# The one-hot rows of the gate matrix, stored one token after another instead of four tokens interleaved

## The chip, the core and the metric

The kernel runs on one core of one Trainium2 chip. The core has a matrix engine (TensorE, PE in the profile; its weight loads are listed apart as PEld), a vector engine (VectorE, DVE), an activation engine (ScalarE, ACT), GpSimd (POOL) and a queue for transfers on SyncE (SP). The engines run side by side, each through its own list of instructions in order, and wait for one another through semaphores. The metric is the device time of one execution in microseconds (us); lower is better.

## The reference

The program is a two-layer decoder on 512 tokens of width 1024. Layer 0 mixes tokens by retention, layer 1 by differential attention; behind each stands an expert feed-forward network with 16384 experts (PEER). Only that network matters here:

```python
sc = jnp.einsum('thpd,hpnd->thpn', q, subkeys)      # two scores per head, 128 keys each
s1, i1 = lax.top_k(sc[:, :, 0], 16)
s2, i2 = lax.top_k(sc[:, :, 1], 16)
cand = s1[..., :, None] + s2[..., None, :]          # the best 16 of these pairs
idx = i1 * 128 + i2                                 # 8 heads x 16 = 128 experts a token
gate = softmax(top)
act = gelu(einsum('ted,td->te', u[idx], xc))
out = einsum('te,ted->td', gate * act, v[idx])
```

So each token uses 128 of 16384 experts, each with a gate. An expert's number is a pair of keys (a, b), both from 0 to 127.

## The kernel before

The 512 tokens are four blocks of 128. Block 0 is done sparsely: the rows of u and v that its tokens chose are gathered from memory, 128 experts at a time, by GpSimd (`sparse_u`, L735 to L743, and `sparse_v`), and VectorE multiplies them. The other 384 tokens are done densely: TensorE multiplies them with all of u and all of v, 128 experts (one value of a) at a time, and a matrix of gates, zero for experts that were not chosen, picks what counts.

That gate matrix is made by `gmat` (L798 to L835), called for each of the three dense blocks in each layer. For one token, its 128 chosen pairs lie along the partitions. `eq` (L820) compares them with 0 to 127 and gives two one-hot rows per pair, one for a and one for b, in bf16. These rows are widened to float32 in the tile `oh`: ScalarE copies the b half (L822), VectorE multiplies the a half with the gate (L823). Then one matmul per token (L827) with `oh[:, 1]` as weights and `oh[:, 0]` as the moving operand sums the 128 pairs into a 128 x 128 gate matrix in PSUM. Four tokens make a round and share a PSUM bank (`b`, of four with the tag "pj"); ScalarE copies the bank out (L830, L832), and every 16 tokens a transfer writes them to memory (L834). A layer has 96 rounds, the kernel 192. `oh` has four buffers (`OHB`) and `eq` two (`EQB`), so VectorE can be up to four rounds ahead of TensorE.

In both `eq` and `oh`, the last axis is the token within the round: element (a, token) lies at 4a + token. In `eq` that lets one comparison with `iota4` make two halves of four tokens at once. In `oh` it means that a matmul, which takes the 128 values of one token, reads one float32 of every four, a step of 16 bytes.

The order of the work around it is made in `peer` (L862 and on). `gates()` runs, for each of the three blocks, `topk_pairs` (L682 to L733: the best 16 pairs of each head, nearly all on VectorE) and then `gmat`. Both are generators that yield a cost, and between the yields `peer` places dense u tiles (`u_tile`, L837: a load, a split of the weights into a high and a low half on ScalarE at L92 and GpSimd at L93, 24 matmuls at L96 to L98 and a gelu at L843) and gathers for block 0 with their product on VectorE (L739, L741). The tiles of a generator step and of `u_tile` alternate by these costs, which are constants and do not depend on the change. The framework's scheduler then places the instructions of each engine. So in this first part of a layer TensorE alternates between rounds of L827 and u tiles, with three long stages of `gmat` and the `topk_pairs` of the next block between them. The second part of a layer multiplies with v and does not use `oh`. The scores' matmuls in `scores` (L793) are float32 too, 128 x 128, with both operands stored without a step.

`topk_pairs` takes its tile `tk_eq` from the same four buffers as `oh`.

Of the kernel before, what the change touches and what calls it, by code (L numbers as in the profile page):

```python
# [18 lines left out]
F32 = mybir.dt.float32  # L19
# [4 lines left out]
AF = mybir.ActivationFunctionType  # L24
OP = mybir.AluOpType
# [3 lines left out]
P = 128  # L29
# [24 lines left out]
OHB = 4  # L54
# [8 lines left out]
def build(tc, I, out):  # L63
    nc = tc.nc
    ctx = ExitStack()
    with ctx:
# [21 lines left out]
        def bank(tag):  # L88
            return psum.tile([P, 512], F32, name=tag, tag=tag, bufs=4 if tag == "pj" else 2)
# [708 lines left out]
        def gmat(kp, idx, gate, t0, gd, G0):  # L798

            ii = kp.tile([P, 2, P], I32, name="g_ii", tag="g_ii")  # L800
            nc.vector.tensor_scalar(out=ii[:, 0, :], in0=idx, scalar1=7, scalar2=None, op0=OP.arith_shift_right)
            nc.vector.tensor_scalar(out=ii[:, 1, :], in0=idx, scalar1=127, scalar2=None, op0=OP.bitwise_and)
            fi = kp.tile([P, 2, P], F32, name="g_if", tag="g_if")
            nc.vector.tensor_copy(out=fi, in_=ii)
            b = bank("rt")
            for i, src in enumerate((fi[:, 0, :], fi[:, 1, :], gate)):
                nc.tensor.transpose(b[:, i * P:i * P + P], src, ident)
            tr = kp.tile([P, 3, P], F32, name="g_tr", tag="g_tr")
            nc.vector.tensor_copy(out=tr.rearrange("p a b -> p (a b)"), in_=b[:, :3 * P])
            ks = kp.tile([P, 2, P], BF16, name="g_ks", tag="g_ks")  # L810
            nc.vector.tensor_copy(out=ks, in_=tr[:, 0:2, :])
            for q in range(P // GT):
                st = kp.tile([P, P - GA * NG0, GT], F32, name="g_st", tag="g_st", bufs=2)
                for r in range(GT // 4):

                    eq = kp.tile([P, 2, P, 4], BF16, name="g_eq", tag="g_eq", bufs=EQB)
                    oh = kp.tile([P, 2, P, 4], F32, name="g_oh", tag="g_oh", bufs=OHB)
                    tk = q * GT + r * 4
                    ts = slice(tk, tk + 4)
                    nc.vector.tensor_tensor(out=eq, in0=iota4[:, None].to_broadcast([P, 2, P, 4]),  # L820
                                            in1=ks[:, :, None, ts].to_broadcast([P, 2, P, 4]), op=OP.is_equal)
                    nc.scalar.activation(oh[:, 1], eq[:, 1], AF.Copy)  # L822
                    nc.vector.tensor_tensor(out=oh[:, 0], in0=eq[:, 0],  # L823
                                            in1=tr[:, 2, None, ts].to_broadcast([P, P, 4]), op=OP.mult)
                    b = bank("pj")
                    for i in range(4):
                        nc.tensor.matmul(b[:, i * P:i * P + P], oh[:, 1, :, i], oh[:, 0, :, i], start=True, stop=True)  # L827
                    b3 = b.rearrange("p (t a) -> p t a", t=4)
                    rs = slice(r * 4, r * 4 + 4)
                    nc.scalar.activation(st[:, :, rs].rearrange("p a t -> p t a"), b3[:, :, GA * NG0:], AF.Copy)  # L830
                    for i in range(NG0):
                        nc.scalar.activation(G0[i][:, t0 // GT + q, :, rs].rearrange("p a t -> p t a"),  # L832
                                             b3[:, :, GA * i:GA * i + GA], AF.Copy)
                nc.sync.dma_start(gd[t0 // GT + q], st.rearrange("p a t -> p (a t)"))  # L834
                yield 6.0  # L835
# [26 lines left out]
        def peer(l, norm, feed, prepare):  # L862
            with tc.tile_pool(name="sp", bufs=1) as sp, tc.tile_pool(name="dp", bufs=1) as dp:
# [6 lines left out]
                with tc.tile_pool(name="p1", bufs=1) as kp:  # L870
# [10 lines left out]
                    with tc.tile_pool(name="tk", bufs=1) as tp:  # L881
                        def gates():
                            for t in range(1, TB):
                                idx = tp.tile([P, P], I32, name="tk_idx", tag="tk_idx", bufs=2)
                                gate = tp.tile([P, 8, 16], F32, name="tk_g", tag="tk_g", bufs=2)
                                yield from topk_pairs(tp, M[t], MI[t], idx, gate)
                                yield from gmat(tp, idx, gate.rearrange("p h k -> p (h k)"), (t - 1) * P, gd, G0)

                        for _ in topk_pairs(tp, M[0], MI[0], idx0, gate0):
                            pass  # L890
                        su = sparse_u(sp, 0, l, idx0, act0)
                        nu, nd, tv, tu = 0, 0, 0.0, -40.0

                        for cost in gates():
                            tv += cost
                            while tu < tv and nu < P:
                                act = u_tile(dp, l, nu)
                                nc.sync.dma_start(ad[nu], act)
                                nu += 1
                                tu += UT  # L900
                                while nd < DOTS * (nu - LAG):
                                    next(su, None)
                                    nd += 1
                                    tv += 1.2
# [130 lines left out]
```

## Time and profile before

| what | value |
|---|---|
| runs of the kernel | 3529.66, 3531.1, 3543.05 us (median 3531.1) |
| the profiled execution | 3544.41 us, of which the span from first to last instruction is 3542.6 us |
| mean granted TensorE clock | 0.980 |
| instructions | 47177 |
| HBM read and written | 692.09 MB and 77.59 MB |

The page of the profile gives the busy time of each engine, a picture of the span in 40 slices of 88.6 us, the chain of work that ended last, and the costliest groups of instructions. A group is named by line, engine, operation and tiles (written<-read), with a count, the time in which any of its instructions ran, the mean length of one in ns, and the idle time of the engine just before them with what ended it. Each float32 matmul of the program shows as two MATMUL records and two LDWEIGHTS records, so the 768 matmuls of L827 are 1536 records. Records of matmuls overlap: the next one starts before the end of the last, so what a matmul costs in a run is the distance from start to start and not the length of a record.

### The profile page before, as it was taken

Reading aid. Unit: us, or ns where it says so; the run is one execution under the profiler, and the core shown is the slowest. Engines: PE = TensorE matmul, PEld = TensorE weight load, DVE = VectorE, ACT = ScalarE, POOL = GpSimd, SP = SyncE. Lnnn points to the kernel's source line nnn. Section 1 sums busy time; section 2 is a strip of 40 time slices with the busy share of each in tenths; the row PEclk is TensorE's granted clock in tenths of the full one; section 3 lists DMA queues with packets and bytes.
Section 4 is the critical chain, followed back from the end, with each engine's and each line's share of the span. In section 5 each row is a group of like instructions: output and inputs, shape, how many; then the busy total and the mean of one; then the engine's idle time right before and its main releaser. Section 6 shows DMA issues by size and latency. Waiting matters only on the chain.

```text
span 3542.6 us, 47177 instructions
## 1 busy us (share of the span) xinstructions
PE 3402.5 (96%) x16666; PEld 3047.2 (86%) x16666; DVE 2590.5 (73%) x4593; ACT 1401.1 (40%) x2436; POOL 1539.4 (43%) x919
## 2 busy tenths in 40 slices
PE   9999998799999999999999999879999999999998
PEld 7888888799999888899888668879999988889997
DVE  4444469987866888997673565998877588888776
ACT  3232333455454333333333543336445433333332
POOL 1110336544644333675533323453555433357653
PEclk9999999899999999999999999989999999999999
DMA  5222224756668999998753213366667799999884
GB/s 203 87 86 84 84 95 132 231 203 218 227 224 291 351 353 360 320 319 275 265 160 91 61 32 94 114 193 227 217 221 244 246 359 359 349 316 335 296 267 136
DMA packets 311486, 772.81 MB, mean 218 GB/s; under 512 B 25808, under 2 KB 153168, under 8 KB 311248
## 3 DMA queue, kind: packets, MB, share of 16 engines
q1 hardware_dynamic: 237520, 501.32, 41.8%
q0 software_dynamic: 73728, 268.47, 22.3%
q8 instruction: 131, 2.15, 0.2%
q14 instruction: 107, 0.88, 0.1%
HBM read 692.09 MB, written 77.59 MB: 217 GB/s over the span
## 4 chain that ended last, share of the span: by engine, by line
PE 79%; DVE 11%; DMA 3%; issue 3%; POOL 2%; ACT 1%; POOLq 0%; SPq 0%; DVEq 0%; ACTq 0%
PE pj L96 12%; PE pj L97 11%; PE pj L98 11%; PE pj L827 10%; PE mu L96 7%; PE mu L98 7%; PE mu L97 7%; PE rt L98 4%; PE rt L97 4%; PE rt L96 4%; DMA vg<-in_v,idx 2%; DVE tk_idf L725 2%; DVE tk_ex L722 1%; DVE scr L741 1%; POOL wl L93 1%
## 5 line engine op out<-in xcount | busy, mean ns | idle before, releaser
L93 POOL TENSOR_TENSOR wl<-wraw,wh 128x1024 fp32r<-128x1024 f32 x316 | 801.8, 2539 | 638.5 <-ACT wh L92 606.0
L92 ACT ACTIVATE wh<-wraw 128x1024 fp32r<-128x1024 f32 x632 | 659.9, 1053 | 704.9 <-issue 270.6
L96 PE MATMUL mu<-xth,wh 128*128 128x384 f32 (+1 forms) x2080 | 713.5, 343 | 23.6 <-ACT uact L843 23.5
L98 PE MATMUL mu<-xth,wl 128*128 128x384 f32 (+1 forms) x2080 | 708.0, 340 | 28.3 <-POOL wl L93 28.3
L97 PE MATMUL mu<-xtl,wh 128*128 128x384 f32 (+1 forms) x2080 | 706.2, 340 | 0.0
L93 DVE TENSOR_TENSOR wl<-wraw,wh 128x1024 fp32r<-128x1024 f32 x316 | 422.7, 1339 | 184.8 <-ACT wh L92 169.4
L739 POOL DMA_INDIRECT ug<-in_u,idx x256 | 312.1, 1219 | 470.1 <-DVE act L741 227.4
L752 POOL DMA_INDIRECT vg<-in_v,idx x256 | 320.7, 1253 | 408.2 <-DVE x L754 225.8
L754 DVE SCALAR_TENSOR_TENSOR x<-vg,wgt,x 128x1024 f32<-128x1024 f32 x256 | 399.2, 1559 | 111.0 <-DMA vg<-in_v,idx 109.6
L92 ACT ACTIVATE wwh<-w 128x384 fp32r<-128x384 f32 x256 | 134.4, 525 | 808.4 <-issue 388.2
L98 PEld LDWEIGHTS mu<-xth,wl 128*128 128x128 f32 x2080 | 397.3, 191 | 31.5 <-POOL wl L93 31.4
L96 PEld LDWEIGHTS mu<-xth,wh 128*128 128x128 f32 x2080 | 398.1, 191 | 30.3 <-ACT uact L843 26.8
L741 DVE CUSTOM_DVE_ANT_0 scr<-ug,x 128x1024 bf16<-128x1024 f32 x256 | 334.6, 1307 | 119.1 <-DMA ug<-in_u,idx 113.2
L97 PEld LDWEIGHTS mu<-xtl,wh 128*128 128x128 f32 x2080 | 398.4, 192 | 3.7
L97 PE MATMUL pj<-wl,wwh 128*128 128x512 f32 x1024 | 399.5, 390 | 0.0
L96 PE MATMUL pj<-wh,wwh 128*128 128x512 f32 x1024 | 399.2, 390 | 0.3 <-ACT wh L92 0.3
L827 PE MATMUL pj<-g_oh 128*128 128x128 f32 x1536 | 376.4, 417 | 23.4 <-DVE g_oh L823 13.8
L98 PE MATMUL pj<-wh,wwl 128*128 128x512 f32 x1024 | 397.8, 389 | 0.0
L827 PEld LDWEIGHTS pj<-g_oh 128*128 128x128 f32 x1536 | 367.1, 331 | 25.3 <-issue 14.3
L823 DVE TENSOR_TENSOR g_oh<-g_eq,g_tr 128x512 f32<-128x512 bf16 x192 | 188.3, 1005 | 98.6 <-PE pj L827 97.9
L93 DVE TENSOR_TENSOR wwl<-w,wwh 128x384 fp32r<-128x384 f32 x256 | 169.7, 664 | 104.5 <-ACT wwh L92 91.9
L98 PEld LDWEIGHTS pj<-wh,wwl 128*128 128x128 f32 x1024 | 192.3, 188 | 40.5
(241 smaller groups left out, 5624.3 us busy)
## 6 DMA issues: line engine op xcount, KB each, us to landing
wraw<-in_ut SPq DMA_DIRECT2D x256, 512.0 KB
wraw<-in_v SPq DMA_DIRECT2D x256, 512.0 KB
gd<-g_st SPq DMA_DIRECT2D x48, 896.0 KB
gl<-gd SPq DMA_DIRECT2D x28, 1536.0 KB
ad<-uact SPq DMA_DIRECT2D x160, 192.0 KB
aact<-ad SPq DMA_DIRECT2D x160, 192.0 KB
wraw<-in_w_in SPq DMA_DIRECT2D x48, 512.0 KB
wraw<-in_peer_w_q SPq DMA_DIRECT2D x32, 512.0 KB
```

Source lines behind the costliest of these rows:

```text
L92: nc.scalar.activation(h, src, AF.Copy)
L93: (eng or nc.vector).tensor_tensor(out=l, in0=src, in1=h.bitcast(F32), op=OP.subtract)
L96: nc.tensor.matmul(o, ah, bh, start=start, stop=False)
L97: nc.tensor.matmul(o, ah, bl, start=False, stop=False)
L98: nc.tensor.matmul(o, al, bh, start=False, stop=stop)
L725: nc.vector.reduce_sum(out=idf[:, hs, :], in_=ex.rearrange("p h c k -> p h k c"), axis=AX.X)
L739: nc.gpsimd.indirect_dma_start(out=u, out_offset=None, in_=I[f"u{l}"], in_offset=bass.IndirectOffsetOnAxis(ap=idx[:, j:j + 1], axis=0))
L741: nc.vector.tensor_tensor_reduce(out=scr, in0=u, in1=X[t], scale=1.0, scalar=0.0, op0=OP.mult, op1=OP.add, accum_out=act[:, j:j + 1])
L752: nc.gpsimd.indirect_dma_start(out=v, out_offset=None, in_=I[f"v{l}"], in_offset=bass.IndirectOffsetOnAxis(ap=idx[:, j:j + 1], axis=0))
L754: nc.vector.scalar_tensor_tensor(out=X[t], in0=v, scalar=w[:, j:j + 1], in1=X[t], op0=OP.mult, op1=OP.add)
L823: nc.vector.tensor_tensor(out=oh[:, 0], in0=eq[:, 0], in1=tr[:, 2, None, ts].to_broadcast([P, P, 4]), op=OP.mult)
L827: nc.tensor.matmul(b[:, i * P:i * P + P], oh[:, 1, :, i], oh[:, 0, :, i], start=True, stop=True)
```

## The change

`oh` gets the shape (2, 4, 128) instead of (2, 128, 4): the 128 values of a token lie side by side. The matmul reads them without a step. ScalarE's copy and VectorE's product write the new order, and so read `eq`, which stays as it was, in the order token after token: a step of four bf16, 8 bytes. The gate in the product is now repeated along the last axis. Counts, types, sizes and buffers of all tiles stay, and on every engine the same instructions stand in the same order before and after.

```diff
-                    oh = kp.tile([P, 2, P, 4], F32, name="g_oh", tag="g_oh", bufs=OHB)
+                    oh = kp.tile([P, 2, 4, P], F32, name="g_oh", tag="g_oh", bufs=OHB)
                     tk = q * GT + r * 4
                     ts = slice(tk, tk + 4)
                     nc.vector.tensor_tensor(out=eq, in0=iota4[:, None].to_broadcast([P, 2, P, 4]),
                                             in1=ks[:, :, None, ts].to_broadcast([P, 2, P, 4]), op=OP.is_equal)
-                    nc.scalar.activation(oh[:, 1], eq[:, 1], AF.Copy)
-                    nc.vector.tensor_tensor(out=oh[:, 0], in0=eq[:, 0],
-                                            in1=tr[:, 2, None, ts].to_broadcast([P, P, 4]), op=OP.mult)
+                    nc.scalar.activation(oh[:, 1], eq[:, 1].rearrange("p a t -> p t a"), AF.Copy)
+                    nc.vector.tensor_tensor(out=oh[:, 0], in0=eq[:, 0].rearrange("p a t -> p t a"),
+                                            in1=tr[:, 2, ts].unsqueeze(2).to_broadcast([P, 4, P]), op=OP.mult)
                     b = bank("pj")
                     for i in range(4):
-                        nc.tensor.matmul(b[:, i * P:i * P + P], oh[:, 1, :, i], oh[:, 0, :, i], start=True, stop=True)
+                        nc.tensor.matmul(b[:, i * P:i * P + P], oh[:, 1, i, :], oh[:, 0, i, :], start=True, stop=True)
```

## The prediction

> **What bounds the kernel now.** I read the page first: which engine is busy, and when.
>
> ```profile
> PE 3402.5 (96%) x16666; PEld 3047.2 (86%) x16666; DVE 2590.5 (73%) x4593; ACT 1401.1 (40%) x2436; POOL 1539.4 (43%) x919
> ...
> PE   9999998799999999999999999879999999999998
> DVE  4444469987866888997673565998877588888776
> ```
>
> TensorE is busy nearly everywhere. VectorE is the only other engine that fills whole slices; the gate stages lie in slices 8 to 13 and 27 to 32, and it has between 6 and 9 tenths there. Busy is not the same as fast, so the second view is the groups of instructions with shapes kept apart: the changed line L827 against L793, the scores' matmuls, which have the same shape and type but operands without a step.
>
> ```profile
> L827 PE MATMUL pj<-g_oh 128*128 128x128 f32 x1536 | 376.4, 417 | 23.4 <-DVE g_oh L823 13.8 <-ACT g_oh L822 9.6
> L793 PE MATMUL rt<-sk,pq 128*128 128x128 f32 x256 | 34.7, 275 | 0.0
> L827 PEld LDWEIGHTS pj<-g_oh 128*128 128x128 f32 x1536 | 367.1, 331 | 25.3 <-issue 14.3 <-ACT g_oh L822 11.0
> L793 PEld LDWEIGHTS rt<-sk,pq 128*128 128x128 f32 x256 | 34.3, 191 | 2.4
> ```
>
> Both the weight load (331 against 191 ns) and the matmul (417 against 275 ns) are longer with the step. What a record costs in a run is its distance to the next, so the third view is the timeline of TensorE, with records of one line merged (start, length, count).
>
> ```profile
> 849.29 7.72 PE L827 MATMUL pj<-g_oh 128*128 128x128 f32 x32
> ```
>
> ```profile
> 449.83 1.50 PE L793 MATMUL rt<-sk,pq 128*128 128x128 f32 x12
> ```
>
> With a step: (7.72 - 0.42) / 31 = 0.235 us from start to start. Without: (1.50 - 0.275) / 11 = 0.111 us. A round has 8 records, so it costs TensorE 1.88 us now.
>
> The fourth view cuts the three gate stages of layer 0 into two stretches each, at the place where VectorE stops being full: length, then busy time of each engine, then clock, DMA share and GB/s. Below it are the records of L827 alone in the same stretches.
>
> ```profile
> core 0: us, PE busy (x) PEld busy (x) DVE busy (x) ACT busy (x) POOL busy (x), PEclk, DMA share, GB/s
> 674.60:716.00 41.40, 41.32 (x201) 41.35 (x201) 41.40 (x73) 27.46 (x61) 19.38 (x12) 0.95 0.79 261
> 716.00:765.80 49.80, 49.80 (x229) 49.80 (x229) 33.22 (x46) 32.54 (x81) 15.11 (x8) 1.00 0.53 188
> 811.50:849.30 37.80, 37.80 (x184) 37.80 (x182) 30.08 (x40) 24.24 (x56) 15.49 (x8) 1.00 0.62 213
> 849.30:920.60 71.30, 71.30 (x354) 71.30 (x354) 41.50 (x54) 40.64 (x91) 34.11 (x20) 1.00 0.69 226
> 963.60:981.30 17.70, 16.65 (x80) 16.20 (x81) 17.70 (x22) 11.42 (x24) 9.65 (x5) 0.75 0.74 244
> 981.30:1092.90 111.60, 111.60 (x563) 111.59 (x562) 56.62 (x74) 61.32 (x135) 52.55 (x30) 1.00 0.64 216
> ```
>
> ```profile
> 716.00:765.80 49.80, 39.09 (x160) 38.05 (x160) 1.00 0.53 188
> 811.50:849.30 37.80, 23.91 (x97) 23.19 (x97) 1.00 0.62 213
> 849.30:920.60 71.30, 38.52 (x160) 37.86 (x160) 1.00 0.69 226
> 981.30:1092.90 111.60, 54.30 (x224) 53.27 (x224) 1.00 0.64 216
> ```
>
> TensorE has no gap in four of the six; L827 is half to three quarters of it. In the first and fifth stretch VectorE has no gap, and TensorE merely keeps up. Fifth, the waits of VectorE over the three stages show who is ahead.
>
> ```profile
> DVE scr L741 <- DMA ug<-in_u,idx: 49.9, 11, 10.2
> DVE g_oh L823 <- PE pj L827: 49.6, 28, 7.9
> DVE g_eq L820 <- ACT g_oh L822: 6.4, 9, 1.8
> ```
>
> VectorE stands still 49.6 us a layer because all four `oh` buffers wait for L827. It is ahead, and TensorE sets the pace.
>
> **The matmuls.** I take 0.111 us as the new distance: same shape, same type, no step. A round falls from 8 x 0.235 to 8 x 0.111 us, that is by 1.0 us. All 192 rounds would give 191 us. The busy times of the groups give less, (376.4 / 1536 - 34.7 / 256) us x 1536 = 168 us, because the scores' records often stand alone and then cost more.
>
> A rule of the Trainium skill bears on this and can be read two ways. The page "SBUF — State Buffer", section "Door 1: The DMA port swizzle", says that memory lines are 16 bytes, that an access pattern needs two hits in a line for full rate, and also that 4 float32 can be strided for free. By the two-hit sentence the old rows, one float32 per 16 bytes, are slow, and the trace agrees (331 and 417 ns against 191 and 275 ns). By the count of 4 they would be at full rate and the change would save nothing; the rows speak against that.
>
> **How much of that reaches the end.** The stages lie in one chain: `topk_pairs` of the next block stands behind `gmat` on VectorE, and everything that follows a stage waits for it. So what a stretch loses in length, the kernel loses. But a stretch cannot become shorter than VectorE's busy time in it. For each stretch I set TensorE's new need (its length less 1.0 us a round) against VectorE's busy time and take the larger:
>
> - 41.40 us, 12 rounds: VectorE 41.4. Gain 0.
> - 49.80 us, 20 rounds (160 records): TensorE 29.8, VectorE 33.2. Gain 16.6.
> - 37.80 us, 12 rounds: TensorE 25.8, VectorE 30.1. Gain 7.7.
> - 71.30 us, 20 rounds: TensorE 51.3, VectorE 41.5. Gain 20.
> - 17.70 us, 4 rounds: VectorE 17.7. Gain 0.
> - 111.60 us, 28 rounds: TensorE 83.6, VectorE 56.6. Gain 28.
>
> Together 72.3 us. Layer 1 has the same stages, 329.9 us in all against 329.6 us, with the same busy times:
>
> ```profile
> sum 329.60, PE 328.48 PEld 328.04 DVE 220.52 ACT 197.61 POOL 146.30; mean PE 54.75 PEld 54.67 DVE 36.75 ACT 32.94 POOL 24.38
> ...
> sum 329.90, PE 328.55 PEld 328.26 DVE 220.42 ACT 197.60 POOL 147.26; mean PE 54.76 PEld 54.71 DVE 36.74 ACT 32.93 POOL 24.54
> ```
>
> So the bound from both engines is 2 x 72.3 = 145 us. I take off 10 us a layer, three estimates. In the second stretch ScalarE has 32.54 us of work beside VectorE's 33.22 us, and two engines that hand work to each other in order don't both run full: 3 us. In the fourth the transfers fill 0.69 x 71.3 = 49.2 us of a stretch that would be 51.3 us long, so the gathers that VectorE waits for (49.9 us a layer now) land later: 3 us. And VectorE enters the `topk_pairs` after the second stage ahead of TensorE by the rounds in the buffers; four rounds shrink by 4 x 1.0 us, and `topk_pairs` starts that much less early: 4 us. That leaves 62 us a layer, **124 us**.
>
> **The two writers of `oh`.** They now read `eq` with a step of 8 bytes. No instruction of the trace does just this. Rows around it:
>
> ```profile
> L823 DVE TENSOR_TENSOR g_oh<-g_eq,g_tr x192: 673/685/3325, 671.2 to 2780.7; 128x512 f32<-128x512 bf16 x192
> L226 DVE TENSOR_TENSOR x<-pj,x 128x512 f32<-128x512 f32 x16 | 11.0, 688 | 21.2 <-PE pj L98 21.2
> L725 DVE TENSOR_REDUCE tk_idf<-tk_ex 128x32 f32<-128x1600 f32 x32 | 93.1, 2943 | 0.0
> L822 ACT ACTIVATE g_oh<-g_eq 128x512 f32<-128x512 bf16 x192 | 120.9, 645 | 67.5 <-DVE g_eq L820 67.2
> L830 ACT ACTIVATE g_st<-pj 128x448 f32<-128x448 f32 x192 | 184.4, 964 | 98.9 <-PE pj L827 98.4
> ```
>
> The low end for VectorE is no change: L823's median of 685 ns for 512 elements is what L226 takes with plain operands, so there is nothing to gain. The high end is L725, which reads float32 with a step of 64 bytes: 2943 / 1600 = 1.84 ns an element, 0.94 us for 512, 0.26 us more a round. That counts where VectorE sets the pace, in the first, second, third and fifth stretch, some 50 rounds a layer: 13 us a layer, 26 us in all. For ScalarE the high end is L830, which writes with a step of 64 bytes: 964 / 448 x 512 = 1.10 us, 0.46 us more; in the second stretch, where ScalarE is as full as VectorE, 20 rounds make 9 us a layer instead of VectorE's 5, so 8 us more in all. I take no change for both: 8 bytes lie much nearer to the plain rows than to 64. By the two-hit rule of that page, two of these reads fall in each line and are free; no row here shows it.
>
> Nothing else moves: the same instructions in the same order on each engine, no transfer added or moved.
>
> **The sum.** 3544.4 us of the profiled execution less 124 us is 3420 us. That execution stands 13 us above the median of the runs, so for a median I predict 3531.1 - 124 = **3407 us**, 3.5% less.
>
> **Rivals.**
>
> *TensorE's whole gain arrives.* VectorE's busy time contains time in which it shares its port with GpSimd (L823 takes from 673 to 3325 ns), which may fall, and gathers may come earlier with TensorE's own pace. Then 168 to 191 us go: 3340 to 3363 us. Against it: in the first stretch VectorE has no gap at all.
>
> *VectorE or ScalarE pays for the step.* With both high ends, 34 us of the 124 are lost, and with denser stalls on top some 60: 3440 to 3470 us.
>
> *The step was not the cause.* If L827 is long for another reason (the page's count of 4 would say so), nothing changes: 3531 us. Against it: L827's records are long even in a run of 32 without a gap, and L793's of the same shape are not.
>
> *Slower: VectorE becomes the bound of all six stretches.* Read with a step, L823 could cost so much that it takes over. VectorE's work in the stretches is 220.5 us a layer, its waits for gathers 49.9 us; 96 rounds fill the rest of 329.6 us when L823 costs 0.62 us more, at 1.30 us or 2.5 ns an element. At 2 us it would be 66 us a layer more, 3663 us. The dearest strided row, L725, has 1.84 ns.
>
> **How the numbers follow.** The forecast, 70%: 3385 to 3435 us. The whole gain, 10%. The writers pay, 14%. No change, 4%. Slower, 2%. The range from 3345 to 3460 us takes in the forecast, most of the first rival and most of the second, and leaves out about 12%. Half a per cent, 18 us, is about what a measurement of this kernel can tell from no change. Faster by more: 94%; within: 4%; slower by more: 2%.
>
> **What would show it.** Right: L827 falls to about 275 ns a matmul and 191 ns a load, 32 records in about 3.7 us; L822 and L823 stay near 645 and 685 ns; VectorE's waits for L827 nearly vanish; TensorE gets gaps in the first half of each stage that it did not have, ended by L823; the first stretch keeps its length and the last shrinks by about 28 us. Wrong: L827 still at 0.235 us from start to start (the step was not the cause), L823's median above 0.9 us (the writers pay), or stretches that keep their length with a wait for gathers or for ScalarE in the place of TensorE.

## The result, and the profile after

The changed kernel takes 3433.1 us (median of 4 runs, 3423.6 to 3438.9) against 3535.8 us before (4 runs, 3529.7 to 3543.1): 0.9706 of the time before, 95% interval 0.9674 to 0.9738. That is 103 us less where 124 us were forecast. The two profiled executions are 113 us apart (3544.41 and 3430.96 us).

The page of the changed kernel: TensorE is busy 164 us less in a span that is 113 us shorter, and VectorE and GpSimd are busy a little more.

```profile
span 3429.2 us, 47177 instructions
PE 3238.1 (94%) x16666; PEld 2873.3 (84%) x16666; DVE 2621.4 (76%) x4593; ACT 1391.2 (41%) x2436; POOL 1565.0 (46%) x919
```

The instructions on `oh`, with shortest, median and longest length in ns:

```profile
L827 PEld LDWEIGHTS pj<-g_oh x1536: 185/192/339, 674.4 to 2671.5; 128*128 128x128 f32 x192
L827 PE MATMUL pj<-g_oh x1536: 271/275/553, 674.4 to 2671.7; 128*128 128x128 f32 x192
L822 ACT ACTIVATE g_oh<-g_eq x192: 654/682/780, 668.4 to 2668.0; 128x512 f32<-128x512 bf16 x192
L823 DVE TENSOR_TENSOR g_oh<-g_eq,g_tr x192: 673/680/3323, 671.0 to 2668.5; 128x512 f32<-128x512 bf16 x192
```

L827 has taken on the scores' lengths, 192 and 275 ns. VectorE's product kept its length (680 against 685 ns) and ScalarE's copy grew by 35 ns (682 against 647). On the timeline of TensorE, 32 records in a run:

```profile
828.12 3.73 PE L827 MATMUL pj<-g_oh 128*128 128x128 f32 x32
```

(3.73 - 0.275) / 31 = 0.111 us from start to start, where 0.235 us stood: the price of a round fell by the 1.0 us that was expected. The same cuts of layer 0 as before, each at the same instruction, with the two times between the stages (third and sixth row) and the passage to the second part (ninth):

```profile
core 0: us, PE busy (x) PEld busy (x) DVE busy (x) ACT busy (x) POOL busy (x), PEclk, DMA share, GB/s
674.40:711.50 37.10, 33.58 (x201) 32.75 (x201) 37.10 (x65) 25.46 (x58) 19.61 (x12) 0.88 0.78 257
711.50:747.20 35.70, 31.12 (x228) 29.89 (x228) 35.60 (x49) 30.81 (x76) 15.16 (x8) 1.00 0.82 278
747.20:798.30 51.10, 39.23 (x208) 38.59 (x208) 50.93 (x49) 16.64 (x30) 34.61 (x17) 0.87 0.64 212
798.30:828.10 29.80, 27.90 (x183) 27.06 (x182) 29.80 (x38) 23.66 (x56) 14.77 (x8) 0.94 0.73 249
828.10:879.30 51.20, 51.20 (x355) 51.20 (x354) 45.96 (x50) 37.43 (x86) 31.14 (x18) 1.00 0.81 279
879.30:930.80 51.50, 40.81 (x221) 39.83 (x219) 42.32 (x38) 14.17 (x29) 37.00 (x19) 0.93 0.70 230
930.80:949.20 18.40, 15.04 (x80) 14.78 (x81) 18.40 (x22) 11.50 (x24) 10.28 (x5) 0.81 0.76 245
949.20:1032.90 83.70, 83.58 (x563) 83.39 (x562) 68.38 (x72) 59.04 (x133) 49.65 (x27) 1.00 0.78 260
1032.90:1079.50 46.60, 42.15 (x211) 38.61 (x210) 28.08 (x37) 17.48 (x29) 21.91 (x14) 0.96 0.82 287
```

Their partners in the kernel before that were not shown yet:

```profile
765.80:811.50 45.70, 37.35 (x207) 36.71 (x206) 45.53 (x45) 13.62 (x21) 31.42 (x16) 0.93 0.66 216
920.60:963.60 43.00, 38.24 (x220) 37.47 (x218) 38.80 (x33) 12.38 (x20) 31.35 (x15) 0.98 0.67 222
1092.90:1132.70 39.80, 39.80 (x211) 37.22 (x210) 29.31 (x37) 16.90 (x26) 18.70 (x12) 1.00 0.90 312
```

Row by row, the six stretches lost 4.3, 14.1, 8.0, 20.1, -0.7 and 27.9 us, together 73.7. The times between the stages gained 5.4 and 8.5 us, the passage to the second part 6.8 us. That leaves 53 us for layer 0. The column of VectorE tells who sets the pace now: 37.10 of 37.10, 35.60 of 35.70, 50.93 of 51.10, 29.80 of 29.80, and 18.40 of 18.40 in the seventh row. In the fifth and the eighth row TensorE is still all but without a gap (51.20 of 51.20, 83.58 of 83.70). VectorE's waits over the same three stages say it again; 49.6 us of waiting for L827 have become 1.0 us.

```profile
DVE scr L741 <- DMA ug<-in_u,idx: 27.6, 11, 6.9
DVE g_oh L823 <- PE pj L827: 1.0, 1, 1.0
```

TensorE's waits at the rounds, and ScalarE's, over the same stages:

```profile
PE pj L827 <- DVE g_oh L823: 11.7, 7, 6.2
PE pj L827 <- ACT g_oh L822: 11.2, 6, 3.6
ACT g_oh L822 <- DVE g_eq L820: 57.4, 33, 10.1
```

The gaps that TensorE got at L827 are ended by VectorE's product and about as often by ScalarE's copy, where the prediction named L823 alone. But ScalarE itself waits for VectorE's comparison, 57.4 us where it was 26.9 us before.

Matching the 16666 records of TensorE one by one between the two executions shows the shift along the program: at most 4 us up to the first gate stage, 60 us at the end of the third, 53 to 55 us from the passage on and through the whole second part, 66 us at the first round of layer 1, 123 us at its last, 115 us behind its passage and 113 us at the end. So layer 1 gave 115 - 66 = 49 us.

The 12 us between the layers' stages are not the change's. Some 3 us arise at the end of the second part and in attention, and nearly all of the rest at one place ahead of the first round of layer 1, where the kernel before happens to wait for a split on GpSimd:

```profile
2348.21 0.69 PE L98 MATMUL mu<-xth,wl 128*128 128x384 f32 x1 [9.81 <-POOL wl L93]
```

Two kernels of the experiments below tell that apart. With a step of 8 bytes, where the rounds are nearly as fast as here, the shift is 57 us after attention and still 57 us at the first round of layer 1; with only the moving operand mended, where they are nearly as slow as before, it grows by 10 us at this place all the same. Such a difference is within what runs of one kernel differ by (13 us before, 15 us after).

### The profile page after: what moved, and what is told of

It reads as the page before. It is cut to its first block, busy times and chain, and to the rows that moved or that the text cites. A ratio compares the mean times of both kernels' runs of the same rounds, so it can differ in the third digit from the quotient of the medians.

```text
span 3429.2 us, 47177 instructions
## 1 busy us (share of the span) xinstructions
PE 3238.1 (94%) x16666; PEld 2873.3 (84%) x16666; DVE 2621.4 (76%) x4593; ACT 1391.2 (41%) x2436; POOL 1565.0 (46%) x919
## 5 line engine op out<-in xcount | busy, mean ns | idle before, releaser
L93 POOL TENSOR_TENSOR wl<-wraw,wh 128x1024 fp32r<-128x1024 f32 x316 | 818.3, 2591 | 491.3 <-ACT wh L92 451.5
L739 POOL DMA_INDIRECT ug<-in_u,idx x256 | 322.9, 1261 | 484.9 <-DVE act L741 234.8
L741 DVE CUSTOM_DVE_ANT_0 scr<-ug,x 128x1024 bf16<-128x1024 f32 x256 | 363.8, 1421 | 112.9 <-DMA ug<-in_u,idx 112.5
L827 PE MATMUL pj<-g_oh 128*128 128x128 f32 x1536 | 197.8, 285 | 48.9 <-DVE g_oh L823 25.5
L827 PEld LDWEIGHTS pj<-g_oh 128*128 128x128 f32 x1536 | 190.1, 200 | 57.5 <-ACT g_oh L822 26.0
L96 PEld LDWEIGHTS pj<-wh,wwh 128*128 128x128 f32 x1024 | 192.2, 188 | 42.2 <-ACT wwh L92 4.1
```

The source lines that it names most:

```text
L93: (eng or nc.vector).tensor_tensor(out=l, in0=src, in1=h.bitcast(F32), op=OP.subtract)
L96: nc.tensor.matmul(o, ah, bh, start=start, stop=False)
L739: nc.gpsimd.indirect_dma_start(out=u, out_offset=None, in_=I[f"u{l}"], in_offset=bass.IndirectOffsetOnAxis(ap=idx[:, j:j + 1], axis=0))
L741: nc.vector.tensor_tensor_reduce(out=scr, in0=u, in1=X[t], scale=1.0, scalar=0.0, op0=OP.mult, op1=OP.add, accum_out=act[:, j:j + 1])
L827: nc.tensor.matmul(b[:, i * P:i * P + P], oh[:, 1, i, :], oh[:, 0, i, :], start=True, stop=True)
```

## The experiments

The main theory is that a step of 16 bytes makes TensorE's reads slow, that the change takes this away in full, and that VectorE's list of work then sets the pace, so that only part of the 191 us arrives. Rivals are that one operand alone was slow, that the step was not the cause, and that something else than VectorE holds the changed kernel back. All times are medians, and each ratio is to runs of the kernel before on the same chip.

### One operand at a time

```diff
-nc.scalar.activation(oh[:, 1], eq[:, 1], AF.Copy)
+nc.scalar.activation(oh1_by_token, eq[:, 1].rearrange("p a t -> p t a"), AF.Copy)
...
-nc.tensor.matmul(b[...], oh[:, 1, :, i], oh[:, 0, :, i], start=True, stop=True)
+nc.tensor.matmul(b[...], oh1_by_token[:, i, :], oh[:, 0, :, i], start=True, stop=True)
```

Here `oh1_by_token` is the half `oh[:, 1]` seen as four rows of 128. The second kernel does the same with `oh[:, 0]` and L823.

> The layout before, but only the weights of L827 (the half that ScalarE writes) lie side by side; the moving operand keeps its step of 16 bytes. Same order of instructions on every engine. Theory A (the two operands are read at the same time, and the slower read sets the distance): L827 stays at about 0.235 us from start to start, its load falls to about 191 ns, the time stays within 10 us of before. Theory B (the reads add up): the distance falls to about 0.17 us, half of the gain, 45 to 60 us less than before. Theory C (only one operand matters): either all of the gain of about 103 us here and none with the moving operand alone, or the other way round.

> The mirror of the run before it: only the moving operand of L827 (the half that VectorE writes) lies side by side, the weights keep their step. Theory A: the matmul record may shorten, the distance stays at about 0.235 us because the load takes 331 ns, the time within 10 us of before. Theory B: 0.17 us and 45 to 60 us less. Theory C: the complement of the run with the weights.

Measured: weights alone 3523.9 us, 0.9952 of before (0.9935 to 0.9968); moving operand alone 3527.5 us, 0.9972 (0.996 to 0.9985). First the kernel with plain weights, then the one with a plain moving operand:

```profile
L827 PEld LDWEIGHTS pj<-g_oh x1536: 186/208/338, 673.6 to 2776.8; 128*128 128x128 f32 x192
845.29 7.41 PE L827 MATMUL pj<-g_oh 128*128 128x128 f32 x32
```

```profile
L827 PEld LDWEIGHTS pj<-g_oh x1536: 308/329/332, 673.3 to 2771.8; 128*128 128x128 f32 x192
845.33 7.56 PE L827 MATMUL pj<-g_oh 128*128 128x128 f32 x32
```

The load with plain weights falls to 208 ns, but 32 records still take 7.41 us, (7.41 - 0.405) / 31 = 0.226 us from start to start; with the other operand it is (7.56 - 0.397) / 31 = 0.231 us (0.405 and 0.397 us are the median lengths of a MATMUL record there). That is theory A: the two reads run side by side and the slower one sets the distance. The gains of 15 and 11 us are a little above the 10 us that it allowed. Half of the change brings a seventh to a ninth of its gain, and neither half can be credited with the 103 us.

### A step of 8 bytes

```diff
-oh = kp.tile([P, 2, P, 4], F32, ...)
+oh = kp.tile([P, 2, 2, P, 2], F32, ...)
...
-nc.tensor.matmul(b[...], oh[:, 1, :, i], oh[:, 0, :, i], ...)
+nc.tensor.matmul(b[...], oh[:, 1, i // 2, :, i % 2], oh[:, 0, i // 2, :, i % 2], ...)
```

The lines of the two writers, left out here, follow the same order.

> Both operands of L827 with a step of 2 float32, 8 bytes: two tokens interleaved instead of four. Same order of instructions. If what costs is that each element lies in another 16-byte line, two elements share one here, and L827 runs at about 0.111 us from start to start as without a step: the time of the changed kernel, about 3433 us. If any step costs, L827 stays slow (0.235 us, about 3535 us), or lies between if the cost grows with the step (0.17 us, 3480 to 3490 us).

Measured: 3438.6 us, 0.9714 of before (0.9697 to 0.973), not to be told from the changed kernel.

```profile
828.00 3.93 PE L827 MATMUL pj<-g_oh 128*128 128x128 f32 x32
L827 PEld LDWEIGHTS pj<-g_oh x1536: 192/196/336, 674.2 to 2678.7; 128*128 128x128 f32 x192
```

With a median record of 0.279 us, (3.93 - 0.279) / 31 = 0.118 us: a step of 8 bytes makes a record 6% longer, one of 16 bytes 112%. So the cost is not that of any step, and it does not grow evenly with the step either. This bears on two sentences of the Trainium skill ("SBUF — State Buffer", section "Door 1: The DMA port swizzle"). That two hits in a 16-byte line are enough agrees with 0.118 us but for the 6%; that 4 float32 can be strided for free, read as a step of 4, does not agree with 0.235 us. That the line is the reason is not shown apart from the length of the step: steps between 8 and 16 bytes, and other places within a line, were not tried.

### Less work on VectorE: short products

```diff
-nc.vector.tensor_tensor_reduce(out=scr, in0=u, in1=X[t], ...)
+nc.vector.tensor_tensor_reduce(out=scr[:, :64], in0=u[:, :64], in1=X[t][:, :64], ...)
```

Both kernels leave out 960 of the 1024 columns of these products, and so most of that sum.

> The kernel before, with VectorE's product of a gathered row (L741) cut to 64 of 1024 columns, so that VectorE has about 1.1 us less a gather and the gathers themselves stay. Part of the sum over columns is left out. In the gate stages TensorE sets the pace before, so only the first stretch of each layer and the times between the stages, where VectorE is full, can shrink: 20 to 60 us less than before. It is the partner of the next run, which has the same order of instructions on every engine.

> The changed kernel with the same cut. If VectorE's pace is what kept the changed kernel from the full 191 us of the matmuls, the distance between this run and its partner grows from about 103 us to 140 to 190 us, and the gate stages run at TensorE's pace. If ScalarE, the transfers or the handover between the parts of a layer hold it back, the distance stays at 90 to 115 us.

Measured: 3493.2 us with the layout before (0.987, 0.9846 to 0.9894), 3405.3 us with the new one (0.9626, 0.9601 to 0.9652). The distance is 88 us; the expected growth did not come. VectorE's waits in the gate stages of layer 0, first with the layout before, then with the new one:

```profile
DVE scr L741 <- DMA ug<-in_u,idx: 99.6, 25, 9.8
DVE g_oh L823 <- PE pj L827: 45.0, 34, 8.0
```

```profile
DVE scr L741 <- DMA ug<-in_u,idx: 106.5, 29, 7.3
DVE g_eq L820 <- ACT g_oh L822: 3.0, 5, 0.8
```

The time that the products gave up went into waiting for the gathered rows: 106.5 us where the changed kernel waits 27.6. The products stand in VectorE's list between the rounds, so a row that lands late holds the rounds behind it just as a long product does. The edit took the work away and left the wait. So shorter products alone do not free the changed kernel. By the expectation 88 us, next to its 90 to 115 us, speaks for something else that holds it back, and the trace shows which: the gathered rows that land late. The rounds in VectorE's list are held up either way; the next pairs take the products and the gathers out of the stages.

### Fewer gathers among the rounds

`DOTS` sets how many gathers of block 0, with their products, are placed in the first part of a layer; the rest follow in the second. Since each is counted with a cost, fewer of them also let fewer u tiles in (60 a layer with 0, 67 with 0.5, 80 with 1.1).

```diff
-DOTS = 1.1
+DOTS = 0.0
```

> The kernel before with DOTS = 0: no gather and no product of block 0 in the first part of a layer, all of them in the second. The partner of the next run, with the same order of instructions on every engine. In the stages TensorE sets the pace as before; the second part takes about 75 gathers a layer more: somewhere between 3500 and 3600 us.

> The changed kernel with DOTS = 0. With short products VectorE waited for the gathers instead, so the cover of that test was incomplete; here VectorE has neither the products nor the waits in the stages. If VectorE's list (products and gathers in order with the rounds) is what holds the changed kernel back, the distance to its partner grows to 140 to 175 us, about 0.9 us for each of the 192 rounds, and the stages run at TensorE's pace. If something else holds it (GpSimd's splits, ScalarE, TensorE's own idle time behind the top-k on VectorE), it stays at 90 to 115 us.

> The changed kernel with DOTS = 0.5, half of the gathers left in the first part. If relief of VectorE in the stages goes on paying, 10 to 30 us below the run with 0.8 (3408 us), that is 3380 to 3400 us; if the second part's transfers are then the limit, at or above 3408 us.

> The kernel before with DOTS = 0.5, partner of the run before it, with the same order of instructions. If TensorE sets the pace there, it gains little in the stages: 3500 to 3540 us, and the distance between the two is above 103 us, at 120 to 155 us.

| DOTS | layout before | new layout | distance |
|---|---|---|---|
| 1.1 | 3535.8 | 3433.1 | 103 |
| 0.5 | 3527.1, 0.9973 of before (0.9961 to 0.9984) | 3380.7, 0.9561 (0.9542 to 0.958) | 146 |
| 0.0 | 3509.6, 0.9928 (0.9908 to 0.9948) | 3362.1, 0.9508 (0.9488 to 0.9528) | 147 |

The row of 1.1 is that of the result. The distance grows by 44 us, as the theory said. But with the products went the gathers, and 20 u tiles a layer with their splits on GpSimd (busy 68.6 us in the three stages of the new layout, where it was 140.6 us), so these runs do not say which of them weighs most. The three stages of layer 0 with DOTS = 0, first in the layout before, then in the new one:

```profile
648.80:724.00 75.20, 74.68 (x333) 74.44 (x334) 51.27 (x68) 55.58 (x136) 14.07 (x5) 0.98 0.35 134
757.80:856.30 98.50, 98.50 (x475) 98.49 (x475) 49.90 (x63) 60.88 (x142) 24.42 (x10) 1.00 0.39 145
885.10:985.10 100.00, 100.00 (x484) 99.99 (x484) 53.35 (x68) 60.47 (x142) 31.97 (x17) 1.00 0.48 170
```

```profile
646.80:698.50 51.70, 46.86 (x333) 44.17 (x334) 48.13 (x67) 50.92 (x128) 11.50 (x5) 0.97 0.45 171
734.50:801.40 66.90, 66.75 (x476) 66.36 (x475) 51.23 (x61) 57.88 (x140) 26.02 (x10) 1.00 0.56 205
836.80:906.50 69.70, 68.32 (x485) 68.00 (x484) 57.04 (x64) 56.35 (x137) 31.11 (x16) 1.00 0.60 210
```

VectorE is full in no stage, TensorE sets the pace of the second and third in both layouts, and these lose 31.6 and 30.3 us, that is 32 rounds of 0.95 to 0.99 us. Only the first is still short of it (23.5 us; ScalarE is busy 50.92 of 51.70 there). The times between the stages, cut by the same rows, grow here too, by 2.2 and 6.6 us.

### Two settings of the changed kernel

```diff
-DOTS = 1.1
+DOTS = 0.8
```

> The changed kernel with DOTS = 0.8 in place of 1.1: about a quarter of the gathers and products of the first part of a layer move to the second part, where VectorE has slack and TensorE is full. If VectorE sets the pace of the stages, their stretches and the times between them lose up to 20 x 1.3 us a layer, and the time is 10 to 45 us below the changed kernel. Against it: the transfers of the second part are near full, and more gathers there may cost it as much; then it is the same as the changed kernel or slower by up to 20 us.

```diff
-                yield 6.0
+                yield 8.0
```

> The changed kernel with 8.0 in place of 6.0 as the cost that the gate stages count for 16 tokens: about 12 more u tiles a layer go into the stages, out of the second part, where each costs TensorE 4.2 us. Where the stages are paced by VectorE, TensorE's idle time takes a tile for nothing: some 10 to 30 us less than the changed kernel. If each tile also brings its product on VectorE and its split on GpSimd, which share a port, the stages grow by as much as the second part shrinks: no change.

Measured: 3408.1 us with DOTS = 0.8 (0.962, 0.9589 to 0.9651), 25 us below the changed kernel, in line with the two pairs. With the cost of 8.0, 98 u tiles a layer go into the first part instead of 80 (12 more were expected), and the time is 3447.9 us (0.9745, 0.9721 to 0.9769), 15 us above the changed kernel's median: the expected gain did not come, and more u tiles beside the rounds are not had for nothing. That each brings a product on VectorE and a split on GpSimd is an argument, not shown by this run alone. The fastest version of the study is the new layout with DOTS = 0: 3362 us, 71 us below the changed kernel.

## Why the prediction was right

The measured 3433 us lies within the 3385 to 3435 us that had a chance of 70%, though close to its upper end: 103 us went where the sum said 124.

**The price of a round** was right: 0.111 us a record, as in the scores, 1.0 us a round.

**The writers** were rightly taken at no change on VectorE. ScalarE's 35 ns more was within the bounds; 192 of them are 7 us. TensorE does wait for its copy now, but ScalarE waits longer for VectorE, as the rows above show.

**The floors of the six stretches** were right, down to which engine would hold each: 72.3 us a layer were worked out, 73.7 us measured. The first stretch, put at nothing, gave 4.3 us, and the second lost 14.1 of its 16.6. Both come from what the floors took as fixed, VectorE's work in a stretch. VectorE is less far ahead after the change, so it does 65 instructions in the first stretch where it did 73, and 49 in the second where it did 46, and these fill 35.60 of its 35.70 us. The 3 us taken off there stood for a hand-over between two full engines, and that is not what happened: ScalarE is busy 30.81 of the 35.70 us, VectorE has no gap. In the fourth and the sixth stretch VectorE's busy time even rose, from 41.50 to 45.96 and from 56.62 to 68.38 us with fewer instructions; that cost nothing where TensorE sets the pace. The deduction of 3 us for late gathers in the fourth was not needed; VectorE's wait for them fell from 49.9 to 27.6 us a layer.

**The step that was too small** is the correction to "what a stretch loses, the kernel loses". The lead of VectorE was counted once, at 4 us; it was lost behind two stages and weighed more. Before, VectorE began the top-k of the next block long ahead of TensorE's last round: its last product of the first stage ended at 756.36 + 0.69 = 757.05, TensorE's last round at 765.8.

```profile
756.36 0.69 DVE L823 TENSOR_TENSOR g_oh<-g_eq,g_tr 128x512 f32<-128x512 bf16 x1 [0.55 <-PE pj L827]
```

```profile
745.43 0.69 DVE L823 TENSOR_TENSOR g_oh<-g_eq,g_tr 128x512 f32<-128x512 bf16 x1
```

After (the second row) it is 746.12 and 747.2: VectorE sets the pace there, and of a lead of 8.75 us 1.08 us are left, 7.7 us less. Behind the second stage the last product ended 14.7 us before TensorE's last round, now 3.4 us. The four rounds that TensorE has left there did shrink by the 4 us of the prediction (7.72 to 3.73 us), but before, TensorE also had 7 us of u tiles to do ahead of them.

Not all of that lead had been used for work. `tk_eq` waits for the same four buffers as `oh`, and behind the first stage VectorE stood still for 4.1 of its 8.8 us of lead:

```profile
759.14 0.99 DVE L719 TENSOR_TENSOR tk_eq<-iota,tk_pb 128x1600 bf16<-128x1600 bf16 x1 [2.10 <-PE pj L827]
762.13 2.32 DVE L719 TENSOR_TENSOR tk_eq<-iota,tk_pb 128x1600 bf16<-128x1600 bf16 x1 [1.99 <-PE pj L827]
```

Behind the second it stood still for 7.0 us, most of it for gathered rows. Such waits shorten with the rounds: from its last product of one stage to its first of the next VectorE took 50.1 and 57.6 us before, and takes 47.4 and 54.8 us now. So 7.7 and 11.3 us less of lead came out as only 5.4 and 8.5 us more between the stages, together 13.9 us in layer 0 instead of 4.

The passage to the second part was not in the sum at all. TensorE comes to it 60 us earlier, and has to wait there for ScalarE and GpSimd, where it waited for nothing before:

```profile
PE pj L96 <- ACT wwh L92: 2.3, 1, 2.3
PE mu L98 <- POOL wl L93: 1.3, 1, 1.3
PE mu L96 <- ACT uact L843: 0.9, 1, 0.9
```

That is 46.60 - 42.15 = 4.5 us, and the same 211 records are busy 42.15 instead of 39.80 us at a granted clock of 0.96 (1.00 before). It cost 6.8 us in layer 0 and, by the matched records, 8 us in layer 1. With DOTS = 0 it cost 4.1 and 3.8 us (in layer 0 the shift goes from 78.6 to 74.5 us).

So layer 0 gave 73.7 - 13.9 - 6.8 = 53 us in place of 62 us. In layer 1 the matched records give 73.7 us in the stages as well, 16.3 us lost between them and 8 us in the passage, that is 49 us. The two layers make 102 us; that this meets the difference of the medians so closely is partly luck, as runs of one kernel differ by more.

**The rivals.** That the whole gain arrives failed on VectorE, as argued against it, and comes within reach only when VectorE is relieved (147 of 191 us; GpSimd and the transfers were relieved with it). That the writers pay, that the step was not the cause and that VectorE makes it slower fell with the lengths above. One reading of the prediction was off without an effect on the sum: the page gives VectorE 5 tenths, not 6 or more, in slice 32.

**What stays open.** Why the gathered rows land late among the rounds (their issue on GpSimd behind the splits, or the transfers themselves) was not taken apart. Nor were the products, the gathers and GpSimd's splits taken out of the stages one at a time with the whole sum left in, so that what holds VectorE's list back most stays open.

## What to carry to other kernels

When an operand of the matrix engine is read with a step, compare its distance from start to start with a plain operand of the same shape and type in the same trace; if both operands have the step, mend both, since half of the repair brought about an eighth of the gain here. Then cost the gain stretch by stretch as the larger of two floors, the engine's new need and the busy time of the next engine, and charge the loss of lead at every place where that next engine goes on to other work. Take the lead from the trace, from the end of the next engine's last instruction to the end of the backlog behind it, and take off what that engine spends of it in waits. A faster engine is worth more after the planner's settings are tried again: the same change was worth 103 us at the old setting and 147 us with the gathers, and the u tiles that go with them, moved out of the stages.

## What the runs showed of the hardware

- TensorE reads float32 at 0.111 us a record of 128 without a step, 0.118 us with a step of 8 bytes and 0.235 us with 16 bytes. With only one operand at 16 bytes it is 0.226 or 0.231 us.
- Reading bf16 with a step of 8 bytes cost VectorE nothing (680 to 685 ns for 512 elements whichever way it read) and ScalarE 35 ns of 647.
- VectorE's comparison L820, which the change doesn't touch, kept its median (684 and 680 ns) while its mean went from 837 to 1069 ns, with single ones up to 3300 ns (2872 before). All 32 that took over 1000 ns ran beside a split on GpSimd (mean 2591 ns), and 20 of the 160 others did; before it was 14 of 14 and 6 of 178. That the split is the reason is likely but not shown: no run took the splits alone away.

```profile
L820 DVE TENSOR_TENSOR g_eq<-iota,g_ks 128x1024 bf16<-128x1024 bf16 x192 | 199.9, 1069 | 0.3
```
